# RWKV-7 and pooling decoder layer: the second step of the unit solve beside the first of the next unit, y's halves crossed, VectorE and SyncE in the order of a play

## The chip, the cores and the metric

The kernel runs on one core of a Trainium2 chip. The metric is the device time of one execution in microseconds (us). TensorE is written PE, its weight loads PEld, VectorE DVE, ScalarE ACT, GpSimd POOL, SyncE SP. SP issues most of the DMAs.

## The reference, cut to what matters

One decoder layer for 1024 prompt rows and 8 x 8 sample rows. The input goes through one projection, whose columns feed an RWKV-7 branch (8 heads of size 64), a pooling branch and two gates; then follow an output projection and an MLP.

```python
h = adaLN(RMSNorm(x), c);  P = h @ w_in          # 1024 -> 1792 + 512 + 2048 columns
# RWKV-7, per head, a state S of 64 x 64:
sa = einsum("vk,k->v", S, -kk_t)
S = S * w_t[None, :] + sa[:, None] * (kk_t * a_t)[None, :] + v_t[:, None] * k_t[None, :]
y_t = einsum("vk,k->v", S, r_t)
o_r = (group_norm(y) + bonus) * g;  o_p = pool(pp)
merged = sig(g_r) * (o_r @ w_br_rwkv) + sig(g_p) * (o_p @ w_br_pool)
x = x + gt * (merged @ w_out)
x = x + gt2 * (square(relu(adaLN(RMSNorm(x)) @ w_ff1)) @ w_ff2)
```

## The kernel before, in words

Features lie on the 128 partitions and the 1088 rows (1024 of the prompt, 64 of the samples) along the free dimension, mostly cut into chunks of 364, 362 and 362 columns. Phase 1 runs to about 745 us: the projection `w_in`, the RWKV branch and the pool. Phase 2 holds the output projections and the MLP.

The large products of fp32 data are made of three products of rounded halves. `weights` loads a block of 128 x 512 into `wraw`, ACT copies it to `whi`, DVE subtracts to get `wlo`; PE then multiplies `hx` by `whi`, its remainder by `whi` and `hx` by `wlo` (`mm<-hx,whi` twice, `mm<-hx,wlo` once per chunk). `whi` and `wlo` have two buffers each. This is the stream, in full 128 x 128 mode of the array.

Between the stream's matmuls stand those of the RWKV branch. It works on four head pairs, f = 0 to 3, one head on each half of the partitions, so its matmuls use 64 x 64 quarters of the array. The sequence is cut into 16 chunks of 64 rows, in two units of 8 (u = 0, 1), and a third unit for the samples. For each head pair come `front` (decays, keys; tiles `wt`, `bk`, `ra`, `uv`, some of them loaded from scratch memory `d_x` by SP), the scores of each unit, an inverse (`iv`, `hv`), and `affine`:

- `first(u)`, line 1130: `z` times `at`, 16 matmuls (each of two passes) on the diagonal quarters, where rows and columns belong to the same head. Its rows in the trace are `w<-at,z`, 32 passes.
- `second(u)`, line 1145: `at` times `ab`, on the off-diagonal quarters (`w<-ab,at`, 32 passes). It gives `ra`, with which `chain` goes on.

The loop at line 1160 makes first(0), second(0), first(1), second(1), each behind a `need` that yields to the stream until its operands and two PSUM buffers "w" are there. `chain` (line 1168) then walks the chunks of a unit: `pn` holds the state's increment, `py` the output y. At each step PE makes `wc<-S,ra` (the state product into `pn`), DVE makes the next S from S, `end` and `pn`, and PE makes `wc<-ra,S` (y, into `py`), both on the diagonal quarters. Over 15 steps for each of four head pairs that is 60 chain steps. At the end of a unit ACT copies `py` to a tile, which SP stores to `d_y` with one DMA (for f = 3 it stays in the tile `y3`). `post` normalizes y with products by `bones` (`w<-wt,kct`) and gives the rows `hx` of the RWKV branch, which `or_job` multiplies at the start of phase 2. `pools` makes four groups of the pooling branch in tiles `d`, `px`.

What sets the order: PE's program is the order in which the code emits its matmuls. A planner sets it (`Pace`, `Need`, `Clocks`): generators of the branch's parts and the stream are advanced by a modelled time, in which every operation of PE, DVE, ACT and SP is booked with a cost. The order on DVE, ACT, POOL and SP is chosen by the framework's scheduler, from the code's dependences and its own cost model. All matmuls are recorded at the helper `mm` (line 359), all instructions of the other engines at a helper (line 187; 393 in the changed kernel, where `mm` is line 573).

Of the kernel before, what the change touches and what calls it, by code (L numbers as in the profile page):

```python
# [78 lines left out]
class Clocks:  # L79
# [5 lines left out]
    def __init__(self, pace):  # L85
        self.pace, self.on = pace, False
        self.busy = {"vector": [], "scalar": [], "gpsimd": [], "sync": []}
        self.seen, self.slots, self.table = {}, {}, 0

# [84 lines left out]

class Engine:
# [5 lines left out]
    def __getattr__(self, op):  # L181
        f = getattr(self.real, op)

        def g(*a, **kw):
            if self.c.on:
                self.c.op(self.name, op, a, kw)
            return f(*a, **kw)  # L187

        return g
# [11 lines left out]
class Pool:  # L201
# [5 lines left out]
    def tile(self, *a, **kw):  # L207
        t = self.pool.tile(*a, **kw)
        if self.c.on and kw.get("tag") and kw["tag"] not in self.free:
            self.c.new(kw["tag"], kw["bufs"], t)  # L210
        return t
# [110 lines left out]
class K:  # L322
# [27 lines left out]
    def mm(self, out, lhsT, rhs, **kw):  # L350
        n, mode = math.prod(rhs.shape[1:]), tuple(32 if v <= 32 else 64 if v <= 64 else 128 for v in (lhsT.shape[0], math.prod(lhsT.shape[1:])))
        if mode != self.mode:
# [4 lines left out]
        self.pace.t += n / 2.4 + 14 if rhs.dtype == F32R else self.took(n, mode)  # L357
        self.product(out, lhsT, rhs)
        return self.nc.tensor.matmul(out, lhsT, rhs, **kw)  # L359
# [22 lines left out]
    def tr(self, out, in_, ident):  # L382
        if self.mode != (P, P):
            self.pace.t += 150 if self.clocks.on else 200
        self.mode = (P, P)
        if self.clocks.on:
            self.pace.t = max(self.pace.t, self.clocks.ready(in_), self.clocks.touch(out, False))
        self.pace.t += 2 * math.prod(ident.shape[1:]) / 2.4 + 3
        self.product(out, in_)
        self.nc.tensor.transpose(out, in_, ident)  # L390
# [734 lines left out]
    def affine(self, f, d):  # L1125
# [4 lines left out]
        def first(u):  # L1130
            Q = d["qs"][u]
            uv, at = Q["uv"], Q["at"]
            pss = [self.ps("w") for _ in range(2)]
            for i in range(8):
                for os in HB[::-1]:
                    self.mm(pss[i // 4][os, i % 4 * 128:(i % 4 + 1) * 128], z[os, 8 * u + i, :], at[os, i, :, :].rearrange("p s j -> p (s j)"),
                            start=True, stop=True)
            for a, ps in enumerate(pss):
                us = slice(4 * a, 4 * a + 4)
                pv = ps.rearrange("p (c s j) -> p c s j", s=2, j=64)  # L1140
                nc.scalar.activation(at[:, us, 0, :], pv[:, :, 0, :], AF.Copy)
                nc.vector.tensor_copy(uv[HB[1], us, 0, :], pv[HB[1], :, 1, :])
                nc.scalar.activation(uv[HB[0], us, 1, :], pv[HB[0], :, 1, :], AF.Copy)

        def second(u):
            Q = d["qs"][u]
            ab, ra, w = Q["ab"], Q["ra"], Q["at"][:, :, 0, :]
            pss = [self.ps("w") for _ in range(2)]
            for i in range(8):
                for h, hs in enumerate(HB):  # L1150
                    os = HB[1 - h]
                    self.mm(pss[i // 4][hs, i % 4 * 128:(i % 4 + 1) * 128], w[os, i, :], ab[os, i, h, :], start=True, stop=True,
                            tile_position=(os.start, hs.start))
            for a, ps in enumerate(pss):
# [5 lines left out]
        for u in range(2):  # L1160
            Q = d["qs"][u]
            yield self.need(z, Q["at"], banks=("w", "w"))
            first(u)
            yield self.need(Q["at"], Q["ab"], banks=("w", "w"))
            second(u)
            self.done.add(("s", f, u))

    def chain(self, f, d):
# [4 lines left out]
        for u in range(2):  # L1173
# [5 lines left out]
            for ps, w, x in ((pn, ab[:, :, :, 64:128], uv), (py, uv, ab[:, :, :, 0:64])):  # L1179
                for i in range(8):  # L1180
                    for h, hs in enumerate(HB):
                        self.mm(ps[hs, i * 64:(i + 1) * 64], w[:, i, h, :], x[:, i, h, :], start=i == 0, stop=False, skip_group_check=True)
            for i in range(8):
# [271 lines left out]
    def phase1(self, ctx):  # L1455
# [42 lines left out]
        self.clocks.on = True  # L1498
        self.pace.split = lambda: self.mode != (P, P)
        self.pace.run(back, [self.chains(), self.heads(), self.pools(), self.or_rows()])  # L1500
        self.clocks.on = False
        self.pace.split = lambda: True
# [706 lines left out]
```

## Time and profile before

| | us |
|---|---|
| runs | 1594.35, 1596.3, 1600.01 |
| median | 1596.3 |
| profiled execution, its own time | 1603.45 |
| its span | 1601.7 |
| PE busy in the span | 1536.2 |
| DVE busy | 1109.6 |
| granted clock of TensorE, mean | 0.988 |

A row of a timeline has the start in us, the duration, the engine, the line, the operation, the output and the inputs (names without buffer numbers), the shape and a count; in brackets stands how long the engine was idle before, and who released it. PE's durations overlap, since matmuls are pipelined: what a block costs is read from the start of one row to the start of the next. A row of the windows has the window, its length, the busy time of PE, PEld, DVE, ACT and POOL (with counts), PE's granted clock, the DMA engines' share and GB/s. A row of the waits has who waited for whom: us in total, times, the longest.

### The profile page before, as it was taken

What the parts mean: (1) busy time and instruction counts of PE and PEld (TensorE: products, weight loads), DVE (VectorE), ACT (ScalarE), POOL (GpSimd) and SP (SyncE); (2) the same over time, 40 slices, a digit from 0 to 9 for tenths busy, and PEclk for the clock granted to TensorE, in tenths of its full rate; (3) what the DMA queues carried; (4) which work ended last, traced back from release to release, by engine and by line L of the source; (5) the groups of instructions that cost most, each with busy time, mean ns of one, the idle gap of its engine ahead of it and who ended that gap; (6) DMA issues with size and microseconds to landing.
All of it is one profiled execution on the core that took longest, in us unless ns stands there. A gap on an engine that the chain in (4) does not pass through costs nothing.

```text
span 1601.7 us, 34054 instructions
## 1 busy us (share of the span) xinstructions
PE 1536.2 (96%) x13777; PEld 1445.8 (90%) x13777; DVE 1109.6 (69%) x1944; ACT 664.1 (41%) x1287; POOL 151.4 (9%) x234
## 2 busy tenths in 40 slices
PE   4999999999998999999999999999999999999997
PEld 2998888988898879989899999999999999999997
DVE  5575658775877487536543797998767796666776
ACT  5454364455334543523222573222334344334652
POOL 3100000000000000012510120000000050000000
PEclk9999999999999999999999999999999999999998
DMA  9142523233333343855875555666445996664654
GB/s 363 62 135 76 181 84 112 80 131 128 95 127 119 99 125 119 304 198 179 305 270 188 194 170 198 226 212 206 144 151 202 400 350 197 210 195 160 227 175 144
DMA packets 136399, 290.05 MB, mean 181 GB/s; under 512 B 36881, under 2 KB 40977, under 8 KB 136241
## 3 DMA queue, kind: packets, MB, share of 16 engines
q1 hardware_dynamic: 129856, 266.75, 48.4%
q10 hardware_dynamic: 4320, 14.00, 2.7%
q0 software_dynamic: 2064, 7.13, 1.3%
q8 instruction: 108, 1.77, 0.4%
q14 instruction: 51, 0.41, 0.1%
HBM read 210.54 MB, written 77.28 MB: 180 GB/s over the span
## 4 chain that ended last, share of the span: by engine, by line
PE 79%; DVE 9%; DMA 6%; issue 2%; ACT 2%; SPq 1%; POOL 0%; DVEq 0%; ACTq 0%; POOLq 0%
PE mm L359 52%; PE w L359 13%; PE wc L359 13%; DVE wt L187 2%; DVE hx L187 2%; DMA hid<-in_w_ff 1%; DVE wlo L187 1%; SPq L187 1%; DMA mg<-in_w_ff 1%; DMA wt<-d_x 1%; DMA hid<-in_w_ada_mlp 1%; DVE hv L187 1%; DMA uv<-d_x 1%; DMA t<-d_th 1%; PE w L390 1%
## 5 line engine op out<-in xcount | busy, mean ns | idle before, releaser
L359 PE MATMUL mm<-hx,whi 128*128 128x362 f32 (+2 forms) x2944 | 690.3, 322 | 9.6 <-ACT px L187 3.6
L359 PEld LDWEIGHTS mm<-hx,whi 128*128 128x128 f32 x2944 | 497.9, 190 | 34.6 <-issue 12.8
L359 PE MATMUL mm<-hx,wlo 128*128 128x362 f32 (+2 forms) x1472 | 464.2, 315 | 4.5 <-DVE wlo L187 3.7
L359 PEld LDWEIGHTS mm<-hx,wlo 128*128 128x128 f32 x1472 | 279.6, 190 | 4.7 <-DVE wlo L187 4.7
L359 PE MATMUL mm<-mg,whi 128*128 128x272 f32 (+2 forms) x1312 | 248.8, 289 | 1.2 <-ACT whi L187 0.7
L359 PEld LDWEIGHTS mm<-mg,whi 128*128 128x128 f32 x1312 | 205.4, 188 | 6.1 <-issue 3.4
L359 PE MATMUL mm<-mg,wlo 128*128 128x272 f32 (+2 forms) x656 | 188.5, 287 | 0.0
L359 PE MATMUL wc<-hx,whi 128*128 128x272 f32 x896 | 170.4, 288 | 0.0
L187 ACT ACTIVATE whi<-hid 128x512 fp32r<-128x512 f32 x128 | 80.5, 630 | 148.5 <-PE mm L359 56.1
L359 PEld LDWEIGHTS wc<-hx,whi 128*128 128x128 f32 x896 | 140.3, 188 | 0.0
L359 PE MATMUL wc<-hx,wlo 128*128 128x272 f32 x448 | 128.9, 288 | 2.3 <-DVE wlo L187 2.3
L359 PEld LDWEIGHTS mm<-mg,wlo 128*128 128x128 f32 x656 | 123.6, 188 | 0.0
L187 DVE TENSOR_TENSOR wlo<-hid,whi 128x512 fp32r<-128x512 f32 x128 | 87.5, 686 | 41.0 <-ACT whi L187 40.3
L187 DVE TENSOR_TENSOR wlo<-wraw,whi 128x512 fp32r<-128x512 f32 x82 | 58.3, 711 | 66.7 <-ACT whi L187 60.6
L187 ACT ACTIVATE whi<-wraw 128x512 fp32r<-128x512 f32 x100 | 62.6, 627 | 90.6 <-PE mm L359 48.6
L359 PE MATMUL w<-hx,whi 128*128 128x272 f32 (+1 forms) x480 | 97.2, 297 | 0.0
L187 POOL TENSOR_TENSOR hx<-hx,rs 128x64 f32<-128x64 f32 x24 | 36.8, 1534 | 568.6 <-DMA mg<-in_w_ff 374.2
L359 PEld LDWEIGHTS wc<-hx,wlo 128*128 128x128 f32 x448 | 84.2, 188 | 2.8 <-DVE wlo L187 2.8
L359 PEld LDWEIGHTS w<-hx,whi 128*128 128x128 f32 x480 | 77.3, 189 | 1.0 <-issue 1.0
L359 PEld LDWEIGHTS mm<-mg,hx 128*128 128x128 f32 x576 | 72.8, 188 | 5.0 <-issue 5.0
L359 PE MATMUL mm<-mg,hx 128*128 128x272 f32 (+2 forms) x576 | 74.7, 289 | 0.0
L187 ACT ACTIVATE px<-mm 128x362 f32<-128x362 f32 (+3 forms) x113 | 46.3, 434 | 63.0 <-PE mm L359 56.4
(289 smaller groups left out, 2323.3 us busy)
## 6 DMA issues: line engine op xcount, KB each, us to landing
t<-d_t SPq DMA_DIRECT2D x56, 544.0 KB, 5.0
hid<-in_w_ff SPq DMA_DIRECT2D x110, 256.0 KB, 4.1
d_t<-hx SPq DMA_DIRECT2D x102, 272.0 KB, 2.5
hid<-in_w_ff SPq DMA_DIRECT2D x42, 512.0 KB, 3.8
wraw<-in_w_in SPq DMA_DIRECT2D x68, 256.0 KB, 2.8
mg<-in_w_ff SPq DMA_DIRECT2D x58, 256.0 KB, 5.4
hid<-in_w_ada_mlp SPq DMA_DIRECT2D x24, 512.0 KB, 5.7
d_th<-px SPq DMA_DIRECT2D x22, 544.0 KB, 3.0
```

Source lines behind the costliest of these rows:

```text
L187: return f(*a, **kw)
L359: return self.nc.tensor.matmul(out, lhsT, rhs, **kw)
L390: self.nc.tensor.transpose(out, in_, ident)
```

## The change

1. In `affine`, for f = 1 to 3, first(0) stands alone, then first(1) and second(0) go together, one pair of matmuls of each in turn, and then second(1). second(0) takes its PSUM from "wc". For f = 0 the order stays.
2. In `chain`, the output halves of `py` are crossed: its matmuls lie on the off-diagonal quarters, while those of `pn` stay on the diagonal ones. They are emitted ahead of DVE's new S. The halves are put right when `py` is read out: two stores of 64 x 512 instead of one of 128 x 512 (f < 3), or two ACT copies of half the partitions (f = 3).
3. A new class, `Ledger`, records every operation of phase 1 with a duration fitted to it, its reads, writes and PSUM or SBUF buffers. At the end of phase 1 `fix` plays them: each engine takes the earliest emitted operation that is ready, PE keeps its order, a load lands 1.68 us after its issue plus its bytes by 400 per ns. The order in which VectorE's operations come in the play, and SyncE's from the 60th on, is then imposed on the two engines by dependences between neighbours that carry no semaphore. ACT and POOL stay with the scheduler.

```diff
+class Ledger:
+    WAIT = {"tensor": 55, "gpsimd": 60}
+    OVER = {"vector": 80, "scalar": 95, "gpsimd": 60}
...
+    def cost(self, eng, op, out, ins, a):
+        n = math.prod(out.shape[1:])
...
+        if "dma" in op:
+            return 380
...
+        if op == "reciprocal":
+            return 100 + 6.3 * n
...
+        return 150 + 1.05 * n + 60 * (cols > 0)
...
+            elif e == "sync" or extra > 99:
+                heapq.heappop(pool[e])
+                if len(landed) > 7:
+                    t = max(t, landed[-8])
+                free[e] = t + 380
+                served = end = max(t + 1680, served) + extra / 400
+                landed.append(end)
...
+    def fix(self, tc):
+        order = self.schedule()
+        for e, k in (("vector", 0), ("sync", 60)):
+            line = [self.ops[i][1] for i in order[e][k:]]
+            for a, b in zip(line, line[1:]):
+                tc.add_manual_dep(b, a.name, mybir.DependencyInfo(mybir.DependencyClass.NoSync, mybir.DependencyReason.DATA), reason="order")
...
     def affine(self, f, d):
-        def first(u):
+        def first(u, share=1.0):
...
                 for os in HB[::-1]:
                     self.mm(pss[i // 4][os, i % 4 * 128:(i % 4 + 1) * 128], z[os, 8 * u + i, :], at[os, i, :, :].rearrange("p s j -> p (s j)"),
-                            start=True, stop=True)
+                            share=share, start=True, stop=True)
+                yield
...
-        def second(u):
+        def second(u, tag="w", share=1.0):
...
-            pss = [self.ps("w") for _ in range(2)]
+            pss = [self.ps(tag) for _ in range(2)]
...
-        for u in range(2):
-            Q = d["qs"][u]
-            yield self.need(z, Q["at"], banks=("w", "w"))
-            first(u)
-            yield self.need(Q["at"], Q["ab"], banks=("w", "w"))
-            second(u)
-            self.done.add(("s", f, u))
+        def beside(*gs):
+            for _ in range(9):
+                for g in gs:
+                    next(g, None)
...
+        yield self.need(z, A[0], banks=("w", "w"))
+        beside(first(0))
+        if f:
+            yield self.need(z, *A, B[0], banks=("w", "w", "wc", "wc"))
+            beside(first(1, 0.55), second(0, "wc", 0.55))
+        else:
+            yield self.need(A[0], B[0], banks=("w", "w"))
+            beside(second(0))
+        self.done.add(("s", f, 0))
+        if not f:
+            yield self.need(z, A[1], banks=("w", "w"))
+            beside(first(1))
+        yield self.need(A[1], B[1], banks=("w", "w"))
+        beside(second(1))
+        self.done.add(("s", f, 1))
...
     def chain(self, f, d):
-            for ps, w, x in ((pn, ab[:, :, :, 64:128], uv), (py, uv, ab[:, :, :, 0:64])):
+            for ps, w, x, HO in ((pn, ab[:, :, :, 64:128], uv, HB), (py, uv, ab[:, :, :, 0:64], HB[::-1])):
                 for i in range(8):
-                    for h, hs in enumerate(HB):
+                    for h, hs in enumerate(HO):
...
+                    for hs, os in zip(HB, HB[::-1]):
+                        self.mm(py[os, at], S[hs, :], ra[hs, i, 0, :], share=0.2, start=False, stop=True, skip_group_check=True,
+                                tile_position=(hs.start, os.start))
                     nc.vector.scalar_tensor_tensor(S1, S, end[:, c:c + 1], pn[:, at], op0=ALU.mult, op1=ALU.add)
-                    for hs in HB:
-                        self.mm(py[hs, at], S[hs, :], ra[hs, i, 0, :], start=False, stop=True, skip_group_check=True)
...
             if f == 3:
-                nc.scalar.activation(self.y3[:, us], py, AF.Copy)
+                for hs, os in zip(HB, HB[::-1]):
+                    nc.scalar.activation(self.y3[hs, us], py[os, :], AF.Copy)
             else:
...
-                nc.sync.dma_start(self.d_y[f][:, us], y)
+                for hs, os in zip(HB, HB[::-1]):
+                    nc.sync.dma_start(self.d_y[f][hs, us], y[os, :])
```

`share` is the part of a matmul's cost that the planner books. What moves in the programs is shown at three places. PE's program at `affine` of f = 1, before (`at_2847`, `ab_2845` are unit 0's, `at_3173`, `ab_3171` unit 1's; `mm` rows are stream; a count stands for passes of two heads):

```order
L359 MATMUL w_4120<-ab_2845,at_2847 64x128 x8
L359 MATMUL w_4121<-ab_2845,at_2847 64x128 x8
L359 MATMUL mm_3960<-hx_217,whi_3931 128x362
...
L359 MATMUL w_4170<-at_3173,z 64x128 x8
L359 MATMUL w_4171<-at_3173,z 64x128 x8
L359 MATMUL wc_4194<-uv_2846,ab_2845 64x64 x16
L359 MATMUL wc_4195<-ab_2845,uv_2846 64x64 x16
L359 MATMUL wc_4194<-S_4228,ra_2742 64x64 x2
L359 MATMUL wc_4195<-ra_2742,S_4228 64x64 x2
L359 MATMUL w_4236<-ab_3171,at_3173 64x128 x8
L359 MATMUL w_4237<-ab_3171,at_3173 64x128 x8
```

And now, at the same place (unit 0's tiles are `at_2903`, `ab_2901`, unit 1's `at_3187`, `ab_3185`):

```order
L573 MATMUL w_4122<-at_3187,z 64x128 x2
L573 MATMUL wc_4126<-ab_2901,at_2903 64x128 x2
L573 MATMUL w_4122<-at_3187,z 64x128 x2
L573 MATMUL wc_4126<-ab_2901,at_2903 64x128 x2
...
L573 MATMUL w_4123<-at_3187,z 64x128 x2
L573 MATMUL wc_4127<-ab_2901,at_2903 64x128 x2
...
L573 MATMUL w_4196<-ab_3185,at_3187 64x128 x8
L573 MATMUL w_4197<-ab_3185,at_3187 64x128 x8
L573 MATMUL wc_4238<-uv_2902,ab_2901 64x64 x16
```

Unit 0's second step and unit 1's first are one block now, and the first chain steps come behind second(1), no longer around it. VectorE's program near 114 to 124 us of the trace of before, at the front of f = 0 (`uv_1188` and `uv_1482` are transposed, `wlo_1130` is the stream's):

```order
L187 STREAM_TRANSPOSE uv_1482<-uv_1482 64x8x64
L187 SCALAR_TENSOR_TENSOR ra_1478<-wt_707,e_1021 128x8x64
L187 TENSOR_TENSOR ra_1478<-wt_1019,e_1021 128x8x64
...
L187 STREAM_TRANSPOSE uv_1482<-uv_1482 64x8x64
L187 TENSOR_TENSOR bk_1025<-wt_706,wt_911 64x9x64 x2
L187 SCALAR_TENSOR_TENSOR bk_1025<-wt_912,wt_911 64x9x64 x2
L187 TENSOR_TENSOR wlo_1130<-wraw_1127,whi_1129 128x512
```

And now:

```order
L393 STREAM_TRANSPOSE uv_1188<-uv_1188 64x8x64
L393 TENSOR_TENSOR wlo_1130<-wraw_1127,whi_1129 128x512
L393 TENSOR_TENSOR wt_706<-wt_706,bk_1025 128x576
L393 SCALAR_TENSOR_TENSOR wt_912<-wt_912,wt_707 128x576
L393 TENSOR_TENSOR bk_1025<-wt_706,wt_911 64x9x64 x2
L393 SCALAR_TENSOR_TENSOR bk_1025<-wt_912,wt_911 64x9x64 x2
```

`wlo_1130` is row 90 of the program, where it was row 103; the transposes of `uv_1482` and the rows of `ra_1478` come behind it. VectorE's program where the chain of f = 2 runs beside the front of f = 3 (577 us of the trace of before):

```order
L187 SCALAR_TENSOR_TENSOR S_6326<-S_6257,end_4470,wc_6018 128x64
L187 SCALAR_TENSOR_TENSOR ra_6411<-wt_6135,e_6354 128x8x64
L187 TENSOR_TENSOR bk_6358<-wt_6134,wt_6250 64x8x64
L187 SCALAR_TENSOR_TENSOR bk_6358<-wt_6251,wt_6250 64x8x64
L187 TENSOR_TENSOR bk_6358<-wt_6134,wt_6250 64x8x64
L187 SCALAR_TENSOR_TENSOR bk_6358<-wt_6251,wt_6250 64x8x64
L187 TENSOR_SCALAR wt_6250<-wt_6250 128x576
L187 TENSOR_SCALAR bk_6358<-wt_6251,hp 128x9x64
L187 TENSOR_TENSOR ra_6411<-wt_6352,e_6354 128x8x64
L187 SCALAR_TENSOR_TENSOR S_6401<-S_6326,end_4470,wc_6367 128x64
```

And now:

```order
L393 SCALAR_TENSOR_TENSOR S_6345<-S_6295,end_4426,wc_6109 128x64
L393 TENSOR_TENSOR hv_6104<-hv_6104,end_4426 128x512
L393 TENSOR_TENSOR bk_6294<-wt_6093,wt_6204 64x8x64 x2
L393 SCALAR_TENSOR_TENSOR bk_6294<-wt_6205,wt_6204 64x8x64 x2
...
L393 SCALAR_TENSOR_TENSOR S_6372<-S_6345,end_4426,wc_6109 128x64
...
L393 SCALAR_TENSOR_TENSOR S_6419<-S_6372,end_4426,wc_6109 128x64
L393 SCALAR_TENSOR_TENSOR ra_6495<-wt_6094,e_6290 128x8x64
...
L393 TENSOR_TENSOR ra_6495<-wt_6288,e_6290 128x8x64
```

S rows now stand between the `bk` rows and ahead of the rows of `ra` that read the loaded `wt_6288`. Elsewhere in the programs: the pool's last group has its DVE rows from `d` to `px` within 14 rows, where they were spread over 25. PE's program has the same 11562 matmuls, 5340 of them in phase 1; there the tiling mode changes 275 times, where it changed 257 times. Of the chain steps, 7 stood beside a second(1) and 2 do now. The last product by `bones` in `post(3)` was 66 stream matmuls ahead of or_job(0), and is directly ahead of it now.

More of the change, by code (lines that the diff above doesn't have):

```diff
@@ L1 @@
+import heapq
 import math
@@ L88, in __init__ @@
         self.seen, self.slots, self.table = {}, {}, 0
+        self.ledger = Ledger()
     def region(self, ap):
@@ L186, in g @@
                 self.c.op(self.name, op, a, kw)
-            return f(*a, **kw)
+            r = f(*a, **kw)
+            if self.c.on:
+                out, *ins = [x for x in list(a) + list(kw.values()) if hasattr(x, "tensor")]
+                ledger = self.c.ledger
+                ledger.add(self.name, r.ins, ledger.cost(self.name, op, out, ins, a), out, ins, math.prod(out.shape) * 4 if "dma" in op else Clocks.TABLE.get(a[2], 0) if op == "activation" else 0)
+            return r
         return g
@@ L208, in tile @@
         t = self.pool.tile(*a, **kw)
+        if kw.get("tag"):
+            self.c.ledger.tile(t.tensor.name, (id(self), kw["tag"]), kw["bufs"])
         if self.c.on and kw.get("tag") and kw["tag"] not in self.free:
@@ L347, in kc, with mm @@
         return self.kct[:, o:o + w]
-    def mm(self, out, lhsT, rhs, **kw):
+    def mm(self, out, lhsT, rhs, share=1.0, **kw):
         n, mode = math.prod(rhs.shape[1:]), tuple(32 if v <= 32 else 64 if v <= 64 else 128 for v in (lhsT.shape[0], math.prod(lhsT.shape[1:])))
-        if mode != self.mode:
+        was = self.mode
+        if mode != was:
             self.pace.t += 150 if self.clocks.on else 200
@@ L356, in mm @@
             self.pace.t = max(self.pace.t, self.clocks.ready(lhsT, rhs), self.clocks.touch(out, False) if kw.get("start") else 0.0)
-        self.pace.t += n / 2.4 + 14 if rhs.dtype == F32R else self.took(n, mode)
+        self.pace.t += n / 2.4 + 14 if rhs.dtype == F32R else self.took(n, mode) * share
         self.product(out, lhsT, rhs)
-        return self.nc.tensor.matmul(out, lhsT, rhs, **kw)
+        r = self.nc.tensor.matmul(out, lhsT, rhs, **kw)
+        if self.clocks.on:
+            ledger = self.clocks.ledger
+            ledger.add("tensor", r.ins, ledger.product(mode, n, rhs.dtype), out, [lhsT, rhs], 92 if mode != was else 0)
+        return r
     def took(self, n, mode):
@@ L387, in tr @@
             self.pace.t = max(self.pace.t, self.clocks.ready(in_), self.clocks.touch(out, False))
-        self.pace.t += 2 * math.prod(ident.shape[1:]) / 2.4 + 3
+        ns = 2 * math.prod(ident.shape[1:]) / 2.4 + 3
+        self.pace.t += ns
         self.product(out, in_)
-        self.nc.tensor.transpose(out, in_, ident)
+        r = self.nc.tensor.transpose(out, in_, ident)
+        if self.clocks.on:
+            self.clocks.ledger.add("tensor", r.ins, 267, out, [in_, ident])
     def weights(self, src):
@@ L1151, in second @@
                     os = HB[1 - h]
-                    self.mm(pss[i // 4][hs, i % 4 * 128:(i % 4 + 1) * 128], w[os, i, :], ab[os, i, h, :], start=True, stop=True,
+                    self.mm(pss[i // 4][hs, i % 4 * 128:(i % 4 + 1) * 128], w[os, i, :], ab[os, i, h, :], share=share, start=True, stop=True,
                             tile_position=(os.start, hs.start))
+                yield
             for a, ps in enumerate(pss):
@@ L1158, in second @@
                 nc.vector.tensor_tensor(ra[:, us, 0, :], ra[:, us, 0, :], pv[:, :, 0, :], op=ALU.add)
-        for u in range(2):
-            Q = d["qs"][u]
-            yield self.need(z, Q["at"], banks=("w", "w"))
-            first(u)
-            yield self.need(Q["at"], Q["ab"], banks=("w", "w"))
-            second(u)
-            self.done.add(("s", f, u))
+        def beside(*gs):
+            for _ in range(9):
+                for g in gs:
+                    next(g, None)
+        A = [d["qs"][u]["at"] for u in range(2)]
+        B = [d["qs"][u]["ab"] for u in range(2)]
+        yield self.need(z, A[0], banks=("w", "w"))
[3 more added lines that the diff above has]
+            beside(first(1, 0.55), second(0, "wc", 0.55))
+        else:
+            yield self.need(A[0], B[0], banks=("w", "w"))
[7 more added lines that the diff above has]
+        self.done.add(("s", f, 1))
     def chain(self, f, d):
@@ L1498, in phase1 @@
         self.clocks.on = True
+        self.clocks.ledger.begin()
         self.pace.split = lambda: self.mode != (P, P)
@@ L1501, in phase1 @@
         self.clocks.on = False
+        self.clocks.ledger.fix(tc)
         self.pace.split = lambda: True
```

159 lines of the change are left out of this document (added).

## The prediction

> **What bounds the kernel now.** I read the page first (busy shares and the chain that ended last), then the windows of phase 1, the waits of TensorE, and the timelines of PE and DVE at the places that the change touches. Two rows of the page and one of the windows give the frame (us; busy time with instruction counts, then granted clock, DMA share, GB/s):
>
> ```profile
> PE 1536.2 (96%) x13777; PEld 1445.8 (90%) x13777; DVE 1109.6 (69%) x1944; ACT 664.1 (41%) x1287; POOL 151.4 (9%) x234
> PE 79%; DVE 9%; DMA 6%; issue 2%; ACT 2%; SPq 1%; POOL 0%; DVEq 0%; ACTq 0%; POOLq 0%
> 120.00:740.00 620.00, 594.46 (x6621) 533.33 (x6620) 420.75 (x783) 272.96 (x577) 43.44 (x103) 0.99 0.39 131
> ```
>
> TensorE is the bound, in phase 1 too: it idles 620.0 - 594.5 = 25.5 us between 120 and 740. So a gain has two sources there: passes of PE that take less time, and those 25.5 us. What PE waits for longest, and three of the places (start, duration, in brackets the idle time before):
>
> ```profile
> PE wc L359 <- DVE S L187: 8.3, 6, 2.6
> ...
> PE mm L359 <- DVE wlo L187: 3.7, 2, 3.3
> ...
> 124.53 0.43 PE L359 MATMUL mm<-hx,wlo 128*128 128x364 f32 x1 [3.30 <-DVE wlo L187]
> ...
> 493.18 0.60 PE L359 MATMUL mm<-hx,whi 128*128 128x362 f32 x2 [3.12 <-ACT px L187]
> ...
> 577.87 0.33 PE L359 MATMUL wc<-S,ra 64*64 64x64 f32 x4 [2.61 <-DVE S L187]
> ```
>
> The reader is to see that three waits, 3.30 + 3.12 + 2.61 = 9.0 us, are a third of the idle time, and that all hang on VectorE (ACT's px at 493 is made from DVE's px).
>
> **The change part by part.**
>
> *Quarters in `affine`.* For f = 1..3, unit 1's first step goes pair by pair beside unit 0's second. What each costs alone, and what happens where a second step already stands beside chain steps:
>
> ```profile
> 206.21 1.97 PE L359 MATMUL w<-at,z 64*64 64x128 f32 x32
> 208.10 1.07 PE L359 MATMUL wc<-kct,wt 128*128 128x18 f32 x8
> ...
> 220.17 0.27 PE L359 MATMUL wc<-S,ra 64*64 64x64 f32 x2
> 220.20 0.33 PE L359 MATMUL w<-ab,at 64*64 64x128 f32 x2
> ...
> 220.40 0.23 PE L359 MATMUL wc<-ra,S 64*64 64x64 f32 x2
> 220.47 1.37 PE L359 MATMUL w<-ab,at 64*64 64x128 f32 x22
> ...
> 221.80 0.23 PE L359 MATMUL wc<-ra,S 64*64 64x64 f32 x2
> ...
> 222.09 0.43 PE L359 MATMUL mm<-hx,whi 128*128 128x362 f32 x1
> ```
>
> A first step of 32 passes advances PE by 208.10 - 206.21 = 1.89 us. From 220.20 to 222.09 a second step (off-diagonal quarters) takes the same 1.89 us although two whole chain steps (diagonal quarters, the same rows of the array; the first of their rows and the last are shown) run inside it. So passes on the other quarters were free there. If that holds for 32 against 32, one of two steps vanishes: 3 x 1.89 = 5.7 us saved; if quarters that share rows exclude each other under this load, 0. I take 5.7, by the row nearest to it. The Trainium skill ("TensorE: Matmul & The Clock Gate", Part 3, "The mechanism") speaks against it: weight loads overlap running matmuls only in other row groups, and matmuls start in strict program order. By that rule the term would be 0; this trace disagrees, with 1.89 us for both together and second-step rows that start among chain steps which the program puts behind them.
>
> Second(0) now takes two wc banks and frees them when `ra` is read out. The chain that wants them next has stream work of PE ahead of it, so I cost that at nothing; without that cover, by the nearest eviction row, two of
>
> ```profile
> L187 DVE COPY uv<-w 64x256 f32<-64x256 f32 x16 | 6.8, 427 | 12.8 <-ACT at L187 12.7
> ```
>
> or 0.9 us, in each of three head pairs.
>
> *Crossed y.* A chain step between stream matmuls, and how the stream resumes:
>
> ```profile
> 233.72 0.33 PE L359 MATMUL mm<-hx,wlo 128*128 128x362 f32 x1
> 233.89 0.50 PE L359 MATMUL mm<-hx,whi 128*128 128x362 f32 x2
> 234.23 0.32 PE L359 MATMUL mm<-hx,wlo 128*128 128x362 f32 x1
> 234.48 0.33 PE L359 MATMUL wc<-S,ra 64*64 64x64 f32 x4
> 234.64 0.28 PE L359 MATMUL wc<-ra,S 64*64 64x64 f32 x4
> 234.86 0.60 PE L359 MATMUL mm<-hx,whi 128*128 128x364 f32 x2
> 235.30 0.33 PE L359 MATMUL mm<-hx,wlo 128*128 128x364 f32 x1
> ```
>
> The state product takes 234.64 - 234.48 = 0.16 us and y 0.22 us. With y in the other quarters both can run together; at most the shorter, 0.165, goes, at least nothing (the gap ahead of the stream stays). I take two thirds, 0.11. Of 60 such steps, 7 stood beside a second(1) before and cost nothing: 53 x 0.11 = 5.8 us saved (bounds 0 and 8.7). The halves are put right at eviction: six more store issues on SyncE, and for f = 3 two copies of half the partitions on ACT instead of one. The stores' readers (`wt<-d_y`) come later than a store's 2.2 us, and ACT is 41% busy: nothing.
>
> *What the array loses.* The planner's times shift, so the stream is cut at other places. By the order, phase 1 has 275 changes of tiling mode where it had 257. The price from the rows above: into the block 234.48 - 234.23 is 0.08 longer than a stream matmul's 0.17; out of it the pair takes 0.44 for 0.34; the whole detour (235.30 - 234.23, less 0.17 and 0.34) is 0.56, of which two pairs' pace of about 0.11 is work, so 0.09 to 0.17 a change. I take 0.15: 18 x 0.15 = +2.7. And only 2 chain steps still stand beside a second(1): 5 more cost what a step now costs, 0.38 - 0.11 = 0.27: +1.35.
>
> *VectorE and SyncE by the play.* Each place must be looked at by itself. The rows on DVE:
>
> ```profile
> 120.69 1.52 DVE L187 TENSOR_TENSOR bk<-wt,wt 64x576 f32<-64x576 f32 x2
> 122.23 1.52 DVE L187 SCALAR_TENSOR_TENSOR bk<-wt,wt 64x576 f32<-64x576 f32 x2
> 123.79 0.69 DVE L187 TENSOR_TENSOR wlo<-wraw,whi 128x512 fp32r<-128x512 f32 x1
> ...
> 576.93 0.69 DVE L187 TENSOR_TENSOR ra<-wt,e 128x512 f32<-128x512 f32 x1 [0.64 <-DMA wt<-d_x]
> 577.54 0.27 DVE L187 SCALAR_TENSOR_TENSOR S<-S,end,wc 128x64 f32<-128x64 f32 x1
> ```
>
> At 124.5 `wlo` stood behind transposes, `ra` and `bk` rows; in the new order it stands 13 rows earlier, right behind the first transpose of that unit. At 577.9 S stood behind four `bk` rows and an `ra` row that waited for a load; now two S rows come ahead of all of these. At 493 the pool's chain from `d` to `px` was spread over 25 rows among inverse and post; now over 14. All three waits should go. Each also drew a stretch of half clock behind it:
>
> ```profile
> 124.00:128.00 4.00, 3.47 (x21) 3.07 (x23) 4.00 (x6) 1.11 (x1) 0.12 (x2) 0.65 0.36 95
> 128.00:132.00 4.00, 4.00 (x27) 3.78 (x24) 2.35 (x5) 1.39 (x6) 0.99 (x1) 0.92 0.92 308
> 492.00:496.00 4.00, 2.82 (x11) 2.82 (x12) 3.57 (x7) 1.81 (x4) 0.00 (x0) 0.73 0.53 202
> 496.00:500.00 4.00, 4.00 (x21) 3.60 (x19) 2.50 (x3) 1.41 (x3) 1.31 (x5) 0.84 0.01 3
> 578.00:582.00 4.00, 4.00 (x26) 1.94 (x25) 4.00 (x9) 2.59 (x6) 1.20 (x2) 0.65 0.16 25
> 582.00:586.00 4.00, 4.00 (x26) 3.88 (x25) 3.92 (x8) 0.00 (x0) 1.09 (x2) 0.92 0.76 269
> ```
>
> Of 8 us, 4 x (0.35 + 0.08) = 1.7 us of clock are lost each time. Together 9.0 + 3 x 1.7 = 14.1 us. The Trainium skill (same page, Part 1, "What's actually happening") lets the clock fall only after a whole idle window of about 3.4 us; by it the 5.1 us of clock would not hang on these waits and the term would be 9.0. Here a gap of 2.61 us was enough, so the rows decide. A new order of 800 VectorE rows will have waits of its own: PE meets them at other times, and one of the old kind is left (for f = 0 to 1, transposes still stand ahead of an S). I take two thirds of 14.1, 9 us saved. The gain's far end is 14.1 plus the other S waits, 8.3 - 2.6 = 5.7: 19.8. The other end is a loss (rival three).
>
> *End of phase 1.* Before, 66 stream matmuls stood between the last group-norm product and or_job(0); now none.
>
> ```profile
> 732.97 0.77 PE L359 MATMUL w<-wt,kct 128*128 128x362 f32 x2
> ...
> 741.68 0.54 DVE L187 TENSOR_TENSOR hx<-wt,hx 128x362 fp32r<-128x362 f32 x1 [0.57 <-ACT hx L187]
> ```
>
> From that product (it enters at 732.97, its successor at 733.30) to the last `hx` lie 742.22 - 733.30 = 8.9 us. or_job(0) needs this `hx` at its 33rd matmul, 33 x 0.166 = 5.5 us in. The rest, 3.4 us, is a new wait; with the waits inside that tail gone it is 1.3. I take 2 (with a half clock behind it, up to 5.1).
>
> **Sum.** -5.7 - 5.8 + 2.7 + 1.35 - 9 + 2 = -14.45 us. The profiled execution took 1603.45 (span 1601.7): 1589.0. It is 7.15 above the median of 1596.3, which I carry over: 1581.9.
>
> **The rivals.**
>
> 1. *The waits only move.* The play's order takes three waits away and gives as much back elsewhere, half clock included. For it: 25.5 us of idle time are made of over a dozen waits, and a new interleaving makes new ones. Against: at all three places the order is better by many rows. The term of 9 is 0: 1590.9.
>
> 2. *Quarters don't run beside each other.* The two steps of 32 would need 2 x 1.89 us interleaved and y would still end 0.22 behind the state product. For it: no row of before shows 32 passes against 32, and free were 16 short passes beside 32. Against: the unbroken 1.89 us. Without 5.7 and 5.8: 1593.4. That is also where the change would not do what it says.
>
> 3. *VectorE stands at loads that the play believes landed* (the slower side). Its whole program is now one chain, so a row that waits for a load holds all behind it: `wlo` for the stream, S for the chain, and with them PE. The play books a load at 1.68 us + bytes/400 per ns: 3.07 for 544 KB, 1.76 for 32 KB. The trace (median us from issue to landing):
>
> ```profile
> wt<-d_x SPq DMA_DIRECT2D x20, 544.0 KB, 4.7
> uv<-d_x SPq DMA_DIRECT2D x64, 32.0 KB, 2.2
> ```
>
> The place is the front of each head pair, where `ra` reads these `wt` and the transposes `uv`. If all are taken at the booked time, DVE stands 20 x 1.63 + 16 x 0.44 = 39.6 us. It turns the result once PE feels half, 14.45 + 4.8 = 19.3. At six tenths, 23.8: 1605.7. Against: the rows behind have slack mostly, since PE waited only 3.7 us for `wlo` in all, and the old order stood at such loads too.
>
> **How the numbers follow.** Forecast 0.60, at 1581.9. Rival one 0.18, two 0.10, three 0.12. A measurement of this kernel can tell about 0.3%, 4.8 us, from no change. The forecast is faster by that; rival one, 5.4 below, lies at the edge and goes half to faster, half to same; two is same, three slower. Faster 0.60 + 0.09 = 0.69, same 0.09 + 0.10 = 0.19, slower 0.12. Range: the forecast with its gains' far ends (8.7 for y, 19.8 for waits) would be 1568; all three far ends at once are unlikely, so low 1570. High 1597 holds rivals one and two, and leaves out the third.
>
> **What would show it right or wrong.** In the changed kernel's timeline, `w<-at,z` and `wc<-ab,at` together in about 1.9 us (3.8 would be rival two); the state product and y of a step starting within 0.1 us of each other, and the stream back 0.27 us after; the three waits at `wlo`, `px`, S gone from PE's waits and idle time in phase 1 near 18 us; a wait for `hx` of 1 to 3 us where or_job(0) starts. Wrong would be: DVE idle for `d_x` loads well above the 9.9 us that its transposes' row has now,
>
> ```profile
> L187 DVE STREAM_TRANSPOSE uv<-uv 64x512 f32<-64x512 f32 x16 | 11.3, 704 | 10.1 <-DMA uv<-d_x 9.9
> ```
>
> with PE waiting behind; phase 2, which the change leaves alone, longer or shorter by over 2 us; or chain steps that still take 0.38.

## The result, and the profile after

The changed kernel takes 1586.67 us (median of 6 runs, 1583.99 to 1591.22), the kernel before 1598.15 us (median of 6, 1594.35 to 1604.17). The ratio is 0.9921, with a 95% interval from 0.9898 to 0.9943: 0.8% faster. The profiled execution of the changed kernel took 1583.99 us, the fastest of its runs, while that of before (1603.45) was near its slowest. So the two traces differ by 19.5 us where the medians differ by 11.5. Of the 19.5, some 5 are half clock in phase 1 (last table of the experiments).

The page and the window of phase 1, as shown of before:

```profile
PE 1526.2 (96%) x13777; PEld 1432.5 (91%) x13777; DVE 1111.3 (70%) x1944; ACT 658.5 (42%) x1285; POOL 147.9 (9%) x234
120.00:740.00 620.00, 601.23 (x6712) 536.76 (x6712) 429.27 (x798) 268.85 (x578) 42.91 (x106) 0.99 0.41 137
```

TensorE idles 620.0 - 601.2 = 18.8 us between 120 and 740, where it was 25.5. The unit solve of f = 3 in the timeline (start, duration): its first rows and its last.

```profile
669.32 0.33 PE L573 MATMUL w<-at,z 64*64 64x128 f32 x2
669.34 0.33 PE L573 MATMUL wc<-ab,at 64*64 64x128 f32 x2
669.48 0.28 PE L573 MATMUL w<-at,z 64*64 64x128 f32 x2
669.50 0.28 PE L573 MATMUL wc<-ab,at 64*64 64x128 f32 x2
...
671.03 0.28 PE L573 MATMUL wc<-ab,at 64*64 64x128 f32 x2
671.23 0.60 PE L573 MATMUL mm<-hx,whi 128*128 128x362 f32 x2
```

Both steps, 64 passes, take 671.23 - 669.32 = 1.91 us. One alone took 1.89. The other two blocks take 2.08 us (f = 2) and 3.01 (f = 1, with a wait of 0.87 inside). And a chain step:

```profile
269.83 0.27 PE L573 MATMUL wc<-S,ra 64*64 64x64 f32 x2
269.84 0.27 PE L573 MATMUL wc<-ra,S 64*64 64x64 f32 x2
269.94 0.22 PE L573 MATMUL wc<-S,ra 64*64 64x64 f32 x2
269.95 0.23 PE L573 MATMUL wc<-ra,S 64*64 64x64 f32 x2
270.11 0.60 PE L573 MATMUL mm<-hx,whi 128*128 128x362 f32 x2
```

y starts 0.01 us after the state product, and the stream is back 0.28 us after the step's start (0.275 in all 14 steps that stand alone between stream matmuls); it was 0.38. TensorE's waits (us in total, times, longest):

```profile
PE wc L573 <- DVE S L393: 2.3, 4, 1.2
PE mm L573 <- DVE px L393: 2.2, 1, 2.2
...
PE mm L573 <- ACT px L393: 1.7, 3, 0.7
...
PE mm L573 <- DVE wlo L393: 1.1, 2, 0.7
```

The three long waits for `wlo`, `px` and S are gone. In their place stands one of 2.2 us, and two at the turn to phase 2:

```profile
650.60 0.60 PE L573 MATMUL mm<-hx,whi 128*128 128x362 f32 x2 [2.23 <-DVE px L393]
...
725.50 0.88 PE L573 MATMUL w<-wt,kct 128*128 128x362 f32 x2 [1.00 <-ACT wt L393]
...
733.33 1.00 PE L573 MATMUL w<-hx,whi 128*128 128x362 f32 x2 [1.49 <-ACT hx L393]
```

VectorE's timeline just before the first of them shows what `px` stood behind:

```profile
648.82 1.29 DVE L393 TENSOR_TENSOR wt<-wt,wt 128x1088 f32<-128x1088 f32 x1 [0.99 <-DMA wt<-d_bv]
650.02 1.41 DVE L393 SCALAR_TENSOR_TENSOR px<-px,mm 128x364 f32<-128x364 f32 x3
```

A row that waits for a load, 0.99 us, then takes 1.29 us, and `px`, which frees the stream's PSUM, comes behind it. This is the third rival's mechanism, at one place. One stretch of half clock is left in phase 1, right after that wait. It is 6.8 us long, where each of the five of before is 3.4 (the column before the last two is the granted clock):

```profile
652.00:656.00 4.00, 4.00 (x72) 3.53 (x72) 0.04 (x1) 1.18 (x2) 0.00 (x0) 0.50 0.94 287
656.00:660.00 4.00, 4.00 (x52) 2.95 (x52) 0.00 (x0) 0.95 (x2) 0.54 (x1) 0.68 0.53 183
```

### The profile page after: what moved, and what is told of

The parts are those of the page before. It is cut to its first block, busy times and chain, and to the rows that moved or that the text cites. A ratio compares the mean times of both kernels' runs of the same rounds, so it can differ in the third digit from the quotient of the medians.

```text
span 1582.2 us, 34017 instructions
## 1 busy us (share of the span) xinstructions
PE 1526.2 (96%) x13777; PEld 1432.5 (91%) x13777; DVE 1111.3 (70%) x1944; ACT 658.5 (42%) x1285; POOL 147.9 (9%) x234
## 4 chain that ended last, share of the span: by engine, by line
PE 48%; DVE 11%; DMA 7%; issue 2%; ACT 1%; SPq 0%; POOL 0%; DVEq 0%; ACTq 0%; POOLq 0%
PE mm L573 32%; PE wc L573 8%; PE w L573 7%; DVE hx L393 4%; DMA hid<-in_w_ff 2%; DVE wt L393 2%; DMA d_t<-hx 1%; DVE wlo L393 1%; DMA mg<-in_w_ff 1%; DMA wt<-d_bv 1%; DMA hid<-in_w_ada_mlp 1%; DVE hid L393 1%; DVE mg L393 1%; DVE sw L393 0%; DMA wraw<-in_w_br 0%
```

## The experiments

The theory: array and order bring about half each. The rivals: the order alone does it, or the array alone. The first two kernels make a square of two by two with the kernel before and the changed one, since TensorE's program depends on the array's part alone and VectorE's order on the play. The play is run anew on each program, so the order imposed on the old program is not, row for row, that of the changed one.

**Array without order** (e1_scheduler_order):

```diff
-        self.clocks.ledger.fix(tc)
```

> The changed kernel without the imposed order: TensorE's program is the changed one, VectorE and SyncE stand as the framework's scheduler puts them. Theory (array and order each bring about half): the array's part stays, about -7 us (quarters -5.7, y -5.5, more mode changes and fewer hidden chain steps +4), the waits of VectorE stay or come back: ratio to the kernel before about 0.996, idle time of TensorE between 120 and 740 us near 25. Rival 1 (the order does it all, the array's gain is eaten by mode changes): 1.000. Rival 2 (the array does it all, the order only moves waits): 0.992, idle time near 19.

Measured: 1603.81 us, ratio 1.0011 (0.9996 to 1.0026). No gain at all. Under the scheduler's order the changed TensorE program runs into longer waits than the old one, the longest of them here:

```profile
124.88 0.47 PE L573 MATMUL mm<-hx,wlo 128*128 128x364 f32 x1 [3.50 <-DVE wlo L393]
...
669.38 0.67 PE L573 MATMUL mm<-hx,whi 128*128 128x362 f32 x1 [6.48 <-DVE px L393]
```

**Order without array** (e2_order_alone): `affine` and `chain` of the kernel before, `Ledger` and `fix` of the changed one. TensorE's program is that of before, row for row.

```diff
-        yield self.need(z, A[0], banks=("w", "w"))
-        beside(first(0))
...
+        for u in range(2):
+            Q = d["qs"][u]
+            yield self.need(z, Q["at"], banks=("w", "w"))
+            first(u)
...
-            for ps, w, x, HO in (..., (py, uv, ab[:, :, :, 0:64], HB[::-1])):
+            for ps, w, x in (..., (py, uv, ab[:, :, :, 0:64])):
```

> The kernel before (its affine and its chain, so its TensorE program) with the imposed order on VectorE and SyncE alone. Theory (half and half): the waits at 124, 493 and 577 us go, a few smaller ones come: -5 to -9 us, ratio 0.995, idle time between 120 and 740 us from 25.5 to about 17. Rival 1 (the order does it all): 0.992. Rival 2 (the order only moves waits): 1.000, idle time near 25.

Measured: 1589.41 us, ratio 0.9924 (0.9900 to 0.9948). The order alone brings what the whole change brings. With e1 this is what the first rival named, but not for its reason: the matmuls do take less time in e1, and longer waits take that back (the table below). The window of e2 of phase 1 shows 620.0 - 603.9 = 16.1 us idle:

```profile
120.00:740.00 620.00, 603.92 (x6713) 543.22 (x6712) 429.25 (x798) 273.94 (x580) 42.92 (x106) 1.00 0.41 137
```

**y uncrossed** (e3_y_uncrossed), with all programs in the order of the changed kernel:

```diff
-            for ps, w, x, HO in (..., (py, uv, ab[:, :, :, 0:64], HB[::-1])):
+            for ps, w, x, HO in (..., (py, uv, ab[:, :, :, 0:64], HB)):
...
-                    for hs, os in zip(HB, HB[::-1]):
+                    for hs, os in zip(HB, HB):
```

(the second in `py`'s products, and in both read-outs).

> The changed kernel with y back on the diagonal quarters; every program keeps its order, the read-out still goes in two halves, not crossed. Theory: a chain step takes 0.378 us again instead of 0.275, some 55 to 60 times: +5.5 to 6 us on the changed kernel, ratio to before 0.9957. Rival (the steps stand where TensorE has slack, or y fills the gap ahead of the stream): the changed kernel's 0.992.

Measured: 1591.78 us, ratio 0.9954 (0.9936 to 0.9973): 0.33% or 5.3 us above the changed kernel's ratio. As expected, though the two intervals overlap.

**One step after the other** (e4_one_after_other):

```diff
-            beside(first(1, 0.55), second(0, "wc", 0.55))
+            for g in (first(1, 0.55), second(0, "wc", 0.55)):
+                beside(g)
```

> The changed kernel with unit 1's first step emitted whole, then unit 0's second step whole, in the same block, instead of pair by pair. Theory (quarters run beside each other only where their matmuls are neighbours in the program): the block takes 3.8 us instead of 1.9, three times: +5.7 us on the changed kernel, ratio to before 0.9957. Rival (TensorE starts the off-diagonal passes early by itself, as it did with two chain steps before): the block takes 1.9 to 2.5 us, ratio 0.992 to 0.993.

Measured: 1599.15 us, ratio 0.9982 (0.9966 to 0.9997). The block for f = 3:

```profile
680.34 1.64 PE L573 MATMUL w<-at,z 64*64 64x128 f32 x26
681.71 0.33 PE L573 MATMUL wc<-ab,at 64*64 64x128 f32 x2
681.81 0.28 PE L573 MATMUL w<-at,z 64*64 64x128 f32 x2
...
682.09 1.58 PE L573 MATMUL wc<-ab,at 64*64 64x128 f32 x26
683.61 0.59 PE L573 MATMUL mm<-hx,whi 128*128 128x362 f32 x2
```

It takes 3.27 us, 1.36 more than pair by pair and between the two expectations, while the time lies above both. TensorE does start the second step early, ahead of the last three pairs of the first, but no further: neighbours in the program run beside each other, and little beyond. The program has all of `w<-at,z` first, so these starts are out of its order; the Trainium skill ("TensorE: Matmul & The Clock Gate", Part 3, "The mechanism") has matmuls start strictly in order, and the trace disagrees at this place too. The three blocks are 1.38, 1.19 and 1.36 us longer, 3.9 together; the rest of the loss (0.61%, 9.7 us) is idle time and clock, since the planner moved TensorE's program as well (the table below).

**Crossed y alone on the old program** (e5_crossed_only): e2 with the crossing, and y booked at full cost, so that TensorE's program stays.

```diff
-                        self.mm(py[os, at], S[hs, :], ra[hs, i, 0, :], share=0.2, start=False, ...
+                        self.mm(py[os, at], S[hs, :], ra[hs, i, 0, :], start=False, ...
```

> The kernel before with the imposed order and with y's halves crossed; the planner books y at full cost, so TensorE's program is the one of before, and affine is that of before. Theory (the array's gain is real, and what it is missing in the whole change is taken by the re-planned TensorE program: 16 more changes to and from the stream's mode, waits at the start of phase 2): a step falls from 0.378 to 0.275, -5.5 us on the order alone, ratio to before 0.989. Rival (time saved in a step comes back as a wait for VectorE's next S): the order alone's 0.992.

Measured: 1588.04 us, ratio 0.9929 (0.9902 to 0.9955). Neither of the two as written: no gain over e2, and not because S came late (TensorE waits 1.1 us for S in all, in e2 1.4). The traces of e2 and then e5 at the same place, the sample rows of f = 2 (`w<-hv,ra`) between two chain steps:

```profile
538.78 0.23 PE L573 MATMUL wc<-ra,S 64*64 64x64 f32 x2
538.81 0.60 PE L573 MATMUL w<-hv,ra 64*64 64x512 f32 x2
538.84 0.22 PE L573 MATMUL wc<-ra,S 64*64 64x64 f32 x2
539.24 0.59 PE L573 MATMUL w<-hv,ra 64*64 64x512 f32 x2
539.33 0.33 PE L573 MATMUL wc<-S,ra 64*64 64x64 f32 x4
```

```profile
538.62 0.27 PE L573 MATMUL wc<-S,ra 64*64 64x64 f32 x2
538.63 0.60 PE L573 MATMUL w<-hv,ra 64*64 64x512 f32 x2
538.73 0.23 PE L573 MATMUL wc<-S,ra 64*64 64x64 f32 x2
539.06 0.28 PE L573 MATMUL wc<-ra,S 64*64 64x64 f32 x4
```

In e2 the next state product starts 0.09 us after the second `w<-hv,ra`, beside it. In e5 the state product runs beside it too, but the crossed y waits until 539.06, 0.43 us after its start. So the crossing takes y out from behind its own state product and puts it behind other work that had been free of it: `w<-hv,ra` lies on the off-diagonal quarters, as the crossed y does. Over phase 1 the rows of chain steps fall from 21.7 to 17.4 us, the rows of `w<-hv,ra` rise from 1.5 to 3.1, and the next neighbours (`w<-hv,ab`, `w<-ra,bk`) by 1.2 together.

**Loads booked as measured, and as landed at once** (e7_loads_as_measured, e8_loads_at_once), with TensorE's program unchanged:

```diff
-                served = end = max(t + 1680, served) + extra / 400
+                served = end = max(t + 2050, served) + extra / 210
```

```diff
-                served = end = max(t + 1680, served) + extra / 400
+                served = end = t + 100
```

> The changed kernel; the play books a load at 2.05 us + bytes/210 per ns, which fits the trace's 2.2 us for 32 KB and 4.7 us for 544 KB, instead of 1.68 us + bytes/400. TensorE's program is the same. Theory (VectorE has slack at the loads; the play's error costs little): the changed kernel's 0.992 within 0.002. Rival (VectorE stands at loads that the play believes landed, and TensorE behind it): 0.988 or less, VectorE's idle time for loads well below that of the changed kernel.

> The changed kernel; the play books every load as landed 0.1 us after its issue, so VectorE's rows that read loads stand as early as they can be wrong. Theory (the error matters only where wlo or S stand behind such a row): +2 to +6 us on the changed kernel, ratio to before 0.994 to 0.996, VectorE idle for loads some 10 us longer. Rival (the order at loads is worth nothing, since SyncE's loads are issued long before they are read): 0.992, no new waits of TensorE. Third rival of the prediction (a whole VectorE chained to a wrong belief): over 1.000.

Measured: e7 1582.92 us, ratio 0.9895 (0.9869 to 0.9921); e8 1610.26 us, ratio 1.0060 (1.0040 to 1.0080). The belief about loads alone moves the time by 27 us, from faster to slower than before. e7 lies between its two expectations; e8 is over 1.000, as the third one has it. The new booking fits the two kinds of load named; the stream's `wraw` of 256 KB, which landed 2.8 us after its issue in the kernel before, it puts at 3.3. VectorE's transposes, with the idle time ahead of them, in the changed kernel, in e7 and in e8:

```profile
L393 DVE STREAM_TRANSPOSE uv<-uv 64x512 f32<-64x512 f32 x16 | 11.3, 704 | 8.2 <-DMA uv<-d_x 7.9
```

```profile
L393 DVE STREAM_TRANSPOSE uv<-uv 64x512 f32<-64x512 f32 x16 | 11.3, 704 | 4.2 <-DMA uv<-d_x 3.8
```

```profile
L393 DVE STREAM_TRANSPOSE uv<-uv 64x512 f32<-64x512 f32 x16 | 11.3, 704 | 14.8 <-DMA uv<-d_x 14.5
```

The transposes' 6.6 us more in e8 are far less than what the time rose by. A load also holds VectorE by way of ACT: e8's longest wait of TensorE in phase 1 ends with `d`, which stands behind a VectorE row that waits 6.02 us for ACT's rows on `wt`, and the first of these had waited 2.11 us for a load of `d_x`:

```profile
367.93 1.39 ACT L393 ACTIVATE wt<-wt,part 128x512 f32<-128x512 f32 x2 [2.11 <-DMA wt<-d_x]
...
369.87 0.69 DVE L393 TENSOR_TENSOR wt<-wt,wt 128x512 fp32r<-128x512 f32 x1 [6.02 <-ACT wt L393]
370.57 0.60 DVE L393 SCALAR_TENSOR_TENSOR d<-w,part,px 128x364 fp32r<-128x364 f32 x1
...
371.22 1.36 PE L573 MATMUL w<-px,plw 128*128 128x298 f32 x2 [5.01 <-DVE d L393]
```

In e7 `px` comes ahead of the row that waits for `d_bv`, at once after VectorE's previous row, and the wait at 650 is gone. A later `px`, behind that row, is waited for in its place, 1.72 us:

```profile
645.54 0.71 DVE L393 STREAM_TRANSPOSE hv<-w 128x512 f32<-128x512 f32 x1
646.18 1.38 DVE L393 SCALAR_TENSOR_TENSOR px<-px,mm 128x364 f32<-128x364 f32 x3
...
661.60 0.60 PE L573 MATMUL mm<-hx,whi 128*128 128x362 f32 x2 [1.72 <-DVE px L393]
```

No half clock follows it; of the 5.7 us by which the trace of e7 is shorter than the change's in phase 1, 3.4 are half clock (the table below).

Since e7's interval overlaps that of the changed kernel, it was run again (e13_loads_again):

> The changed kernel with loads booked as measured, a second time, since its interval (0.9869 to 0.9921) overlaps that of the changed kernel (0.9898 to 0.9943). Theory (the better fit takes the waits for px and wlo out of this program): ratio to before 0.990 again, and no half-clock stretch between 120 and 700 us. Rival (its first measurement was a good draw): 0.992 to 0.994.

Measured: 1582.63 us, ratio 0.9896 (0.9874 to 0.9919), the same, and no half clock between 120 and 700 us. Its six runs and those of e7 (1580.03 to 1585.43) lie with their medians 4 us below the changed kernel's, though its interval too overlaps the changed kernel's.

**The planner at full cost** (e9_shares_one): `share` left at 1 in `affine` and `chain`.

```diff
-            beside(first(1, 0.55), second(0, "wc", 0.55))
+            beside(first(1), second(0, "wc"))
...
-                        self.mm(py[os, at], S[hs, :], ra[hs, i, 0, :], share=0.2, start=False, ...
+                        self.mm(py[os, at], S[hs, :], ra[hs, i, 0, :], start=False, ...
```

> The changed kernel; the planner books the crossed y and the paired steps at full cost, as if nothing ran beside. TensorE's program falls between the two: 268 mode changes (275 in the change, 257 before), and 39 stream matmuls stand again between the last group-norm product and or_job(0). Theory (the re-planned program eats the array's gain): 7 changes by 0.15 and 2.5 us of waits at the start of phase 2 less, -3 us on the changed kernel, ratio to before 0.990. Rival (the program's place makes no difference): 0.992.

Measured: 1591.10 us, ratio 0.9937 (0.9916 to 0.9957). Fewer mode changes and a longer cover at the end of phase 1 brought nothing, and the ratio lies above both expectations; new waits came (22.4 us idle, table below).

**The better loads on the old program** (e10_order_alone_loads): e2 with e7's line.

```diff
-                served = end = max(t + 1680, served) + extra / 400
+                served = end = max(t + 2050, served) + extra / 210
```

> The order alone on the TensorE program of before (affine and chain of before), with loads booked as measured (2.05 us + bytes/210). Beside the changed kernel with these loads (0.9895) it tells what the array's part is worth under the better order. Theory (what the array saves is mostly handed back in this program: 8.6 us saved in the rows of steps and quarters, some 6 of it returned): 0.991. Rival 1 (the order does it all): 0.9895. Rival 2 (the array's full 7.5 us come through once the waits are gone): 0.994.

Measured: 1593.14 us, ratio 0.9955 (0.9937 to 0.9972). Here the line that helped the changed program did not help, and the array's part is worth 0.6% (0.9955 against e7's 0.9895, intervals apart). That is nearest to the second rival. But e10's new order also made a wait for `hv` longer, 2.82 us where e2 has 1.54, with half clock behind it:

```profile
505.12 1.11 PE L573 MATMUL w<-iv,hv 32*32 32x32 f32 x80 [2.82 <-DVE hv L393]
```

**VectorE alone** (e6_vector_only):

```diff
-        for e, k in (("vector", 0), ("sync", 60)):
+        for e, k in (("vector", 0),):
```

> The changed kernel with the order imposed on VectorE alone; SyncE stands as the framework's scheduler puts it. Theory (VectorE's order holds only with the loads in the order that the play saw): VectorE stands at loads that now come later, ratio to before 0.995 to 1.000, its idle time before transposes for loads over 10 us. Rival (SyncE's order is worth nothing): 0.992.

Measured: 1590.01 us, ratio 0.9941 (0.9925 to 0.9957), between the two. VectorE's idle time for loads before its transposes is 10.6 us, where the change has 7.9. VectorE's row that reads `d_bv` now waits longer, and TensorE's wait for `px` behind it is 4.87 us instead of 2.23:

```profile
654.13 1.29 DVE L393 TENSOR_TENSOR wt<-wt,wt 128x1088 f32<-128x1088 f32 x1 [3.68 <-DMA wt<-d_bv]
655.35 1.41 DVE L393 SCALAR_TENSOR_TENSOR px<-px,mm 128x364 f32<-128x364 f32 x3
```

**f = 0 as well** (e12_f0_too): e7 with the pairing for all four head pairs.

```diff
-        if f:
+        if True:
             yield self.need(z, *A, B[0], banks=("w", "w", "wc", "wc"))
...
-        if not f:
+        if False:
             yield self.need(z, A[1], banks=("w", "w"))
```

> The changed kernel with loads booked as measured, and the paired steps for f = 0 as well. Theory: the fourth pair saves 1.9 us, and two chain steps lose their place beside second(1), +0.55: -1.3 us, ratio to before 0.9887. Rival (TensorE's program moves behind it and new waits come): 0.990 to 0.993.

Measured: 1602.76 us, ratio 1.0019 (1.0003 to 1.0036). The fourth pair saves its 1.9 us, but TensorE's program moves behind it, and waits of 2.6, 3.7, 4.7 and 2.9 us come, as large as the ones that the change took away. VectorE's idle time for loads doesn't foretell this: before the transposes it is 5.3 us here, less than in the change. The three largest sums of TensorE's waits in e12, the solitary one at the start aside:

```profile
PE w L573 <- ACT wt L393: 9.0, 5, 3.7
PE w L573 <- DVE wt L393: 5.2, 5, 1.6
PE mm L573 <- DVE px L393: 4.7, 1, 4.7
```

**All traces side by side.** For each, the last 6740 passes of TensorE up to the start of or_job(0): their time, TensorE's idle time in it, the time lost to half clock (half of TensorE's busy time in the stretches of half clock), and what remains as work. The last column is the measured ratio. What comes ahead of these passes takes 104 to 107 us, in e8 109.

| TensorE's program, order | span | idle | clock | work | ratio |
|---|---|---|---|---|---|
| before, scheduler | 640.1 | 25.5 | 8.5 | 606.0 | 1 |
| before, play (e2) | 625.0 | 16.1 | 1.7 | 607.2 | 0.9924 |
| before with crossed y, play (e5) | 624.3 | 17.0 | 1.7 | 605.6 | 0.9929 |
| before, play with measured loads (e10) | 626.7 | 16.1 | 3.4 | 607.2 | 0.9955 |
| changed, scheduler (e1) | 639.7 | 30.2 | 10.5 | 599.0 | 1.0011 |
| changed, play (the change) | 622.7 | 17.1 | 3.4 | 602.2 | 0.9921 |
| changed, play, VectorE only (e6) | 627.6 | 20.5 | 6.1 | 601.1 | 0.9941 |
| changed, play with measured loads (e7) | 617.0 | 15.5 | 0.0 | 601.6 | 0.9895 |
| the same again (e13) | 616.3 | 14.0 | 0.0 | 602.3 | 0.9896 |
| changed, y uncrossed (e3) | 627.0 | 17.8 | 3.4 | 605.8 | 0.9954 |
| one after the other (e4) | 633.9 | 21.7 | 6.5 | 605.7 | 0.9982 |
| changed, loads at once (e8) | 641.2 | 29.5 | 9.5 | 602.2 | 1.0060 |
| shares of one (e9) | 630.5 | 22.4 | 6.8 | 601.3 | 0.9937 |
| f = 0 too (e12) | 636.4 | 29.2 | 7.2 | 600.0 | 1.0019 |

The work falls by 5.0 us from e2 to the change, by 5.6 from e10 to e7, and by 7.0 from before to e1: the array's gain is there each time. One and the same program shows work of 599.0 to 602.3 us (the change, e1, e6, e7, e8, e13), so these differences are good to some 3 us. Idle time and clock decide what becomes of the gain: they take 6.7 us back from before to e1 (+4.7 and +2.0), 2.7 from e2 to the change (+1.0 and +1.7), and add 4.0 to it from e10 to e7.

## Why the prediction was right, and where its steps were off

The time lies in the range, and its forecast of -14.45 us stands against -11.5 measured, inside the interval (-9 to -16). The forecast time of 1581.9 is 4.8 us below the measured 1586.67; 1.9 of them come from the kernel before, whose median was 1598.15 in this comparison. Phase 2 (848.3 and 848.6 us to the last matmul) and VectorE's idle time before its transposes (7.9 us for loads, 9.9 before) show none of the signs named as wrong.

- **Quarters: right.** Two steps in 1.91 us, as the saving of 5.7 us for three needs it. The blocks of f = 2 and f = 1 took 2.08 and, without a wait of 0.87 us for `d` in its middle, 2.14: 0.4 us more than three times 1.91.
- **Crossed y: the size of a step right** (0.275 us, 0.27 forecast), **the cover wrong.** The step counted 7 hidden chain steps, those beside a second(1); steps also stood beside `w<-hv,ra` and its neighbours, and there the crossing costs (`w<-hv,ra` itself rises from 1.5 to 2.6 us). Chain steps and both unit steps together fell from 50.6 to 41.8 us, 8.8, where 5.7 + 5.8 - 1.35 = 10.15 was forecast.
- **What the array loses: near its size, its reason not shown.** From e2 to the change these rows fall by 8.5 us and the work by 5.0, from e10 to e7 by 8.3 and 5.6, from before to e1 by 8.5 and 7.0: 3.5, 2.7 and 1.5 were handed back. +2.7 for mode changes was the forecast, to which `w<-hv,ra` adds 1.1; no run changes the number of mode changes alone. The net of the array was to be -7.5 and is -5.0 to -7.0.
- **The order: right in its places, too small in its size.** All three waits went, and idle time between 120 and 740 fell to 18.8 (near 18 was named). On the old program the order alone is worth 0.76%, 12 us, where 9 was taken. In the traces the idle time falls by 9.5 us and the loss to half clock by 6.8 there: all five stretches of before are gone, two of which (at 197 and 354 us) stood at waits that the term had not counted, and one came at 396.
- **End of phase 1: right**, 1.00 + 1.49 = 2.5 us where 2 stood.
- **The step that failed is the sum itself.** It adds the array's part and the order's as if each kept its worth. They don't: the array brings 0 under the scheduler's order (e1) and nothing measurable under the change's own (0.9921 against 0.9924), but 0.6% under e7's. That the result agreed is to this extent luck: one term was too large and the other too small.

The rivals. The first (waits only move) is refuted for the play's order by e2, and holds for the array's part in e1. The second (quarters don't run beside each other) is refuted by the rows. The third (VectorE at loads that the play believes landed) is real and has its turning point between the change and e8; the change itself pays a little of it, the 2.23 us at 650 with 3.4 us of half clock behind, for which e7 pays 1.72. Its price in the prediction, 23.8 us, is close to the 22 us by which e8 lies above the change by the ratios, but e8 books the loads far shorter than the change does, so this is no check of that sum.

Left open: why the array's part is worth 0.6% under one order and nothing under the other. The table shows where it goes (idle time, clock), not a rule by which one could foresee it. Untested is the plain rival that any new order draws waits of its own: each program was run with two or three planned orders, and none was varied in a way that should not matter, to see by how much the time scatters from that alone. So the 0.6%, and what e7 gains over the change, can be in part such a draw.

## What to carry to other kernels

Where one engine is full and the others are issued in a fixed order, a saving on the full engine is worth what the others' order lets through: make the two-by-two of old and new order under old and new program before crediting either. If an order is planned from durations, take them from the trace, loads above all; here loads booked 0.4 and 1.6 us too short went with 0.25% on the changed program, within overlapping intervals, and with nothing on the old one, while booking them as landed at once cost 1.4%. And before moving work to free quarters, look at what already ran there.

## What the runs showed of the hardware

Passes on diagonal and off-diagonal quarters run wholly beside each other, 64 in the time of 32 (1.91 us against 1.89), though they share the array's rows, but only if they are near each other in the program: of 32 passes queued behind 32 others, 6 started early. A pass of 512 columns (`w<-hv,ra`) holds those on its own quarters for 0.43 us.

The granted clock falls to half for 3.4 us, which costs up to 1.7 us, or for two or three times that in a row (6.8 us at 652 in the change, 10.2 at 668 in e1). No length of wait alone decides on it: in e2 one such time stood at 396 us behind a wait of 0.81, while in e7 waits of 1.53 and 1.72 us drew none. Over the passes of the table, the kernels with no wait above 2 us (e2, e5, e7, e13) had at most one of 3.4 us, those whose longest lies between 2 and 3 us (the change, e3, e4, e9, e10) two to four, and those with a wait above 3 us (before, e1, e6, e8, e12) four to seven.

Phase 2, which no kernel changed, took between 846.5 and 852.6 us in the 14 traces, from the start of or_job(0) to the end of the last matmul. That spread is as large as most differences looked for here.
